# Turning softmax probabilities with VectorE and DRAM transfers instead of TensorE in a two-layer decoder trunk

## The chip, the core and the metric

The kernel runs on one core of a Trainium2 chip. The metric is device microseconds of one execution, from the core's first instruction to its last, with what lies around it. The core has five engines with queues of their own: TensorE (PE in the profile, with its weight loads as PEld), VectorE (DVE), ScalarE (ACT), GpSimd (POOL) and SyncE (SP), and 16 DMA engines that all queues share.

## The reference

Two pre-norm residual layers on one sequence of 256 tokens with 1024 features, in float32. Layer 0 mixes tokens by causal attention with forget gates, layer 1 by block-sparse attention with a learned relative bias, which for 256 tokens is one causal block. After each mixer come a SwiGLU feed-forward part of width 2816 and a gated per-layer embedding; a last RMS norm closes.

```python
probs = jax.nn.softmax(logits, axis=-1).astype(v.dtype)      # 16 heads, 256 queries, 256 keys
return jnp.einsum('bhqk,bhkd->bhqd', probs, v)               # 64 features of a head
...
h = h + _merge_heads(o) @ fox_w_o[j]
u = _rmsnorm(h, ffn_norm_g[i])
gu = u @ ffn_w_in[i]
h = h + (jax.nn.silu(gu[..., :D_FF]) * gu[..., D_FF:]) @ ffn_w_out[i]
gate = jax.nn.sigmoid(_rmsnorm(h, ple_norm_g[i]) @ ple_w_gate[i])
h = h + gate * (p[i] @ ple_w_up[i])
```

## The kernel before

Weights stream from DRAM once, in pieces of 128 partitions by 1024 values ("half", called by "blocks"; "gapped" reads a piece with a gap, 1080 values). SyncE issues the load into a tile "raw" (six buffers). ScalarE rounds it into "whi" (L163, L181), VectorE subtracts to get the remainder "wlo" (L165, L182); both have six buffers. A product is three matmuls, whi by x-hi, whi by x-lo and wlo by x-hi (mm3, L91 to L93), so that float32 is kept.

The 16 heads are worked in eight pairs, 0 to 7; a pair is 128 features. In attention a loop over j = 0, 2, 4, 6 does this on TensorE: it projects pairs j and j+1 (queries and keys, 96 matmuls, "pq"), and between the projections it does the attention steps of earlier pairs.

- scores (L506): query by key products of a pair ("sp"), then on VectorE the bias and the row minimum (L528), on ScalarE the exponential (L532), on VectorE the reciprocal (L535) and the scaling (L538). The probabilities of a pair lie in a tile "e" (four buffers), 128 queries by 2 heads by 384 columns: 128 keys for the first half of the queries, 256 for the second.
- transposes (L544): the value product needs keys on the partitions, so TensorE turns every 128 by 128 square of e (three a head, six a pair, L551) into a PSUM bank "pp", and ScalarE copies it to "pt" (L556).
- values (L559): pt by v ("po", L565 and L567), then "split" writes hi and remainder of the pair's output (o, L284 on ScalarE and L285 on VectorE).
- wo (L602): the output projection, in eight pieces of weights; piece (hf, c) needs the outputs of pairs 2c and 2c+1. wo(0, 0) and (1, 0) come behind the last scores.

The framework puts each engine's instructions in order ahead of the run, from what is ready by its own estimate, with the order of the program as priority; issue_after keeps named instructions behind others on their engine. On the chip each engine then works strictly in that order and waits where an operand is late. A new tile waits until the tile that held its buffer has been read for the last time.

GpSimd has almost nothing to do in attention, and no transfer is issued by it.

The steps of the last part of attention before, in the order of TensorE: projections of pairs 6 and 7, transposes of 3 and 4, values of 1 and 2, values of 3, scores of 5 and 6, scores of 7, wo(0, 0) and wo(1, 0), transposes of 5, wo(0, 1), transposes of 6 and 7, wo(1, 1), values of 4 and 5, values of 6 and 7, the rest of wo.

Of the kernel before, what the change touches and what calls it, by code (L numbers as in the profile page):

```python
# [27 lines left out]
F32 = mybir.dt.float32  # L28
F32R = mybir.dt.float32r
AF = mybir.ActivationFunctionType  # L30
ALU = mybir.AluOpType

P = 128
S = 256
# [4 lines left out]
NP = H // 2  # L39
# [10 lines left out]
WARM = 8  # L50
RAW = 6
RVW = 384


LINE = 64
# [17 lines left out]
def trunk(ctx: ExitStack, tc: tile.TileContext, xg, wx, xr, pt, w, cst, gf, rel, hot, rvm, out):  # L73
    nc = tc.nc
    one = ctx.enter_context(tc.tile_pool(name="one", bufs=1))
    work = ctx.enter_context(tc.tile_pool(name="work", bufs=2))
    tiny = ctx.enter_context(tc.tile_pool(name="tiny", bufs=2))
    ps = ctx.enter_context(tc.tile_pool(name="ps", bufs=8, space=bass.MemoryType.PSUM))
    dram = ctx.enter_context(tc.tile_pool(name="dram", bufs=1, space=bass.MemoryType.DRAM))
# [7 lines left out]
    mm = nc.tensor.matmul  # L87
# [184 lines left out]
    rr = tiny.tile([2 * BUCKETS, P], F32R, bufs=1, name="rr")  # L272
    ht = work.tile([2 * BUCKETS, RVW], F32, tag="e", bufs=4, name="ht")
    hot2 = work.tile([2 * BUCKETS, RVW], F32R, tag="e", bufs=4, name="hot2")
    rm = work.tile([H, RVW], F32, tag="e", bufs=4, name="rm")

# [4 lines left out]
    v = one.tile([P, 2, D], F32, name="v")  # L281
# [106 lines left out]
    def moba_bias():  # L388

        pb = bank("pb")  # L390
        mm(pb[:, :RVW], rr, hot2, start=True, stop=True)
        rv = work.tile([H, RVW], F32, tag="e", bufs=4, name="rv")
# [33 lines left out]
    def attention(layer, nm, mid, early, nf):  # L426
        vb = [bank(f"v{layer}_{b}") for b in range(4)]
        rest, ahead = None, []
        for c in range(4):
            wt = [early.pop(0) if early else half() for _ in range(2)]  # L430
            for kk in range(2):
                hi, lo = wt[kk]
                k = 2 * c + kk
                if layer == 0:
                    got = enter(vb, nm.k(k), wt[kk], k)
                for t in range(2 * layer):
                    for hf in range(2):
                        cols = slice(hf * HC, (hf + 1) * HC)
                        got = tokens(vb[2 * t + hf], nm.k(k), t, (hi[:, cols], lo[:, cols]), k == 0, k == KT - 1)
# [37 lines left out]
        qk, sm = {}, {}  # L477
# [3 lines left out]
        def project(j, a):  # L481
            if ahead:
                hi, lo = ahead.pop(0)
            elif j > 2 and (j % 2 == 0 or layer and j == 5) and a == 0 or layer and j == 4:
                hi, lo = gapped()
            else:
                hi, lo = blocks(ENTRY if layer and j in (0, 2) and a == 0 else ())
            if a == 0:
                pq[j] = bank(f"pq{layer}_{j}")
            bk = pq[j]  # L490
            for k in range(KT):
                mm3(bk[:, a * S:(a + 1) * S], (hi[k], lo[k]), nm.k(k),
                    start=(k == 0), stop=(k == KT - 1))
            if a == 0:
                return
            del pq[j]
            t = work.tile([P, 2, S], F32, tag="qkt", bufs=3, name=f"qkt{layer}_{j}")
            nc.vector.tensor_tensor(t.rearrange("p a s -> p (a s)"), bk,
                                    nm.row.rearrange("p a s -> p (a s)"), op=ALU.mult)

            th = work.tile([P, 3 * P], F32R, tag="qkh", bufs=3, name=f"qkh{layer}_{j}")
            tl = work.tile([P, 3 * P], F32R, tag="qkl", bufs=3, name=f"qkl{layer}_{j}")
            split(th, tl, t.rearrange("p a s -> p (a s)")[:, P:])
            qk[j] = t, th, tl

        def scores(*js):  # L506

            rows = [slice(s * DH, (s + 1) * DH) for s in range(2)]
            heads = [(2 * j + s, d, qk[j], bank(f"sp{layer}_{2 * j + s}")) for j in js for s, d in enumerate(rows)]
            for _, d, (t, _, _), sp in heads:  # L510
                mm(sp[:, 0:P], t[d, 0, 0:P], t[d, 1, 0:P], start=True, stop=add is None, skip_group_check=True)
            for n, (q, k) in enumerate(((1, 1), (1, 2), (2, 1))):
                for _, d, t, sp in heads:
                    got = mm(sp[:, P:3 * P], t[q][d, 0:P], t[k][d, P:], start=False, stop=(n == 2 and add is None),
                             skip_group_check=True)
            if add:
                for i, _, _, sp in heads:
                    got = add(i, sp)
            sl = (slice(0, P), slice(P, 3 * P))
            for n, j in enumerate(js):  # L520
                del qk[j]
                e = work.tile([P, 2, 3 * P], F32, tag="e", bufs=4, name=f"e{layer}_{j}")

                mn = tiny.tile([P, 2, 2, 2], F32, tag="mn", bufs=4, name=f"mn{layer}_{j}")
                for s in range(2):
                    i, _, _, sp = heads[2 * n + s]
                    for q, b in enumerate(bias(i)):
                        nc.vector.tensor_tensor_reduce(e[:, s, sl[q]], sp[:, sl[q]], b, 1.0, 3.0e38,  # L528
                                                       ALU.add, ALU.min, mn[:, 0, s, q:q + 1])
                for s in range(2):  # L530
                    for q in range(2):
                        nc.scalar.activation(e[:, s, sl[q]], e[:, s, sl[q]], AF.Exp, scale=-1.0,  # L532
                                             bias=mn[:, 0, s, q:q + 1], accum_out=mn[:, 1, s, q:q + 1])
                rc = tiny.tile([P, 2, 2], F32, tag="rc", bufs=4, name=f"rc{layer}_{j}")
                nc.vector.reciprocal(rc, mn[:, 1])  # L535
                for q in range(2):
                    at = e[:, :, sl[q]]
                    nc.vector.tensor_tensor(at, at, rc[:, :, q:q + 1].to_broadcast(list(at.shape)), op=ALU.mult)  # L538
                sm[j] = e
            return got  # L540

        pts = {}

        def transposes(j, tag="pt"):  # L544

            e = sm.pop(j)
            for s in range(2):
                i = 2 * j + s
                pp = bank(f"pp{layer}_{i}")
                for q in range(3):  # L550
                    got = nc.tensor.transpose(pp[:, q * P:(q + 1) * P], e[:, s, q * P:(q + 1) * P], ident)  # L551
                if tag == "pt":
                    pts[i] = work.tile([P, 3 * P], F32, tag="pt", bufs=4, name=f"pt{layer}_{i}")
                else:
                    pts[i] = work.tile([P, 2 * S], F32, tag="fp", bufs=4, name=f"pt{layer}_{i}")[:, 0:3 * P]
                nc.scalar.activation(pts[i], pp[:, 0:3 * P], AF.Copy)  # L556
            return got

        def values(*js):  # L559

            pos = [bank(f"po{layer}_{j}") for j in js]
            heads = [(slice(s * DH, (s + 1) * DH), slice((2 * j + s) * DH, (2 * j + s + 1) * DH), pts.pop(2 * j + s), po)
                     for j, po in zip(js, pos) for s in range(2)]
            for d, c, t, po in heads:
                mm(po[d, :S], v[:, 0, c], t[:, 0:S], start=True, stop=False, skip_group_check=True)  # L565
            for d, c, t, po in heads:
                got = mm(po[d, P:S], v[:, 1, c], t[:, S:], start=False, stop=True, skip_group_check=True)  # L567
            for j, po in zip(js, pos):
                split(oh[:, j], ol[:, j], po[:, :S])
            return got  # L570


        homes = ("pt", "fp") if layer else ("fp", "pt")
        for j in range(0, NP, 2):
            for i in (j, j + 1):
                project(i, 0)
                project(i, 1)
            if j == NP - 2:
                for i in (NP - 5, NP - 4):
                    transposes(i, homes[0])  # L580
                values(NP - 7, NP - 6)
                values(NP - 5)
                scores(NP - 3, NP - 2)
                end = scores(NP - 1)
            else:
                turned = layer == 1 and j == 4
                if turned:
                    for i in range(j - 3, j - 1):
                        transposes(i, "fp")
                if j >= 4:  # L590
                    values(*range(max(j - 5, 0), j - 3))
                got = scores(*range(max(j - 1, 0), j + 1))
                if j >= 2 and not turned:
                    for i in range(max(j - 3, 0), j - 1):
                        transposes(i)
            if layer == 0 and j == 0:
                with tc.issue_after(got.ins):
                    moba.extend(moba_bias())
# [7 lines left out]
        def behind(ins, *parts):  # L606
            with tc.issue_after(ins.ins):
                for a in parts:
                    wo(*a)

        behind(end, (0, 0), (1, 0))
        behind(transposes(NP - 3, homes[1]), (0, 1))
        transposes(NP - 2, homes[1])
        behind(transposes(NP - 1, homes[0]), (1, 1))
        values(NP - 4, NP - 3)
        behind(values(NP - 2, NP - 1), (0, 2), (1, 2), (0, 3))
        for hf in range(2):
            if hf:
# [232 lines left out]
    for layer in range(2):  # L851
# [5 lines left out]
        got = []  # L857
# [120 lines left out]
```

## Time and profile before

| what | value |
|---|---|
| median of 3 runs | 648.08 us (647.97 to 648.86) |
| the profiled execution | 648.17 us, span 646.4 us |
| TensorE clock granted | 0.999 |
| TensorE busy | 638.6 us, 99% of the span |
| VectorE, ScalarE, GpSimd busy | 455.0, 374.6, 10.6 us |
| DMA | 124.23 MB, mean 192 GB/s |

The span reaches from the first to the last instruction in the profile. TensorE's busy time is modelled from pipelined matmuls, so what a group of matmuls costs is read from the starts in the chain or the timeline and not from the mean duration of one.

### The profile page before, as it was taken

To read this page: it belongs to the slowest core of one execution; us is meant where nothing else is said; L and a number is where in the kernel's file an instruction comes from. 1 tells how busy PE (TensorE), PEld (TensorE's weight loads), DVE (VectorE), ACT (ScalarE), POOL (GpSimd) and SP (SyncE) were. 2 spreads that over 40 slices of the span, in tenths; PEclk is the share of its full clock that TensorE was granted. 3 is DMA by queue.
4 is the path that set the end of the run, shared out by engine and by line. 5 is a ranking of instruction groups with operands and counts; after the bars stand their busy time and mean duration, and the time that the engine had idled before them with its cause. 6 is when DMAs were issued, how large, how long until landed. Compare 5 with 4: busy or idle time off the path is not lost.

```text
span 646.4 us, 13196 instructions
## 1 busy us (share of the span) xinstructions
PE 638.6 (99%) x5373; PEld 617.8 (96%) x5373; DVE 455.0 (70%) x733; ACT 374.6 (58%) x635; POOL 10.6 (2%) x23
## 2 busy tenths in 40 slices
PE   9999999999999999999999999999999999999995
PEld 7899999999999999999989999999999999999985
DVE  7789875786666666659895888577666666666675
ACT  6686675754444445448665677666444444454763
POOL 0100000000000000000000000000000000000000
PEclk9999999999999999999999999999999999999999
DMA  9855544398765566565577554436666666665501
GB/s 341 306 197 185 159 128 154 104 328 277 249 201 196 192 194 215 184 206 191 195 242 280 175 166 135 131 106 212 215 196 195 197 198 197 199 210 195 166 1 65
DMA packets 36092, 124.23 MB, mean 192 GB/s; under 512 B 3936, under 2 KB 6592, under 8 KB 36032
## 3 DMA queue, kind: packets, MB, share of 16 engines
q1 hardware_dynamic: 35600, 122.77, 57.9%
q8 instruction: 42, 0.69, 0.4%
q10 hardware_dynamic: 432, 0.62, 0.3%
q14 instruction: 18, 0.15, 0.1%
HBM read 122.30 MB, written 4.22 MB: 196 GB/s over the span
## 4 chain that ended last, share of the span: by engine, by line
PE 97%; issue 2%; POOL 0%; POOLq 0%; DVE 0%; DVEq 0%
PE gu L91 12%; PE gu L92 12%; PE gu L93 12%; PE fo L93 6%; PE fo L91 6%; PE fo L92 6%; PE pq L91 5%; PE pq L93 5%; PE pq L92 5%; PE v L422 4%; PE wo L91 2%; PE wo L93 2%; PE wo L92 2%; PE pp L551 2%; PE pg L91 2%
## 5 line engine op out<-in xcount | busy, mean ns | idle before, releaser
L165 DVE TENSOR_TENSOR wlo<-raw,whi 128x1024 fp32r<-128x1024 f32 (+1 forms) x166 | 201.0, 1217 | 85.0 <-ACT whi L163 79.4
L163 ACT ACTIVATE whi<-raw 128x1024 fp32r<-128x1024 f32 x164 | 172.4, 1059 | 122.6 <-issue 52.6
L91 PE MATMUL gu<-g,whi 128*128 128x256 f32 x704 | 194.9, 277 | 0.0
L92 PE MATMUL gu<-g,whi 128*128 128x256 f32 x704 | 194.7, 277 | 0.0
L93 PE MATMUL gu<-g,wlo 128*128 128x256 f32 x704 | 194.5, 276 | 0.0
L93 PEld LDWEIGHTS gu<-g,wlo 128*128 128x128 f32 x704 | 132.3, 188 | 0.0
L92 PEld LDWEIGHTS gu<-g,whi 128*128 128x128 f32 x704 | 132.2, 188 | 0.1
L91 PEld LDWEIGHTS gu<-g,whi 128*128 128x128 f32 x704 | 132.2, 188 | 0.0
L93 PE MATMUL fo<-fp,wlo 128*128 128x256 f32 x352 | 97.4, 277 | 0.0
L91 PE MATMUL fo<-fp,whi 128*128 128x256 f32 x352 | 97.3, 276 | 0.0
L92 PE MATMUL fo<-fp,whi 128*128 128x256 f32 x352 | 97.3, 276 | 0.0
L182 DVE TENSOR_TENSOR wlo<-raw,whi 128x1080 fp32r<-128x1080 f32 x44 | 56.4, 1282 | 42.0 <-ACT whi L181 41.3
L91 PE MATMUL pq<-g,whi 128*128 128x256 f32 x256 | 71.3, 279 | 0.0
L181 ACT ACTIVATE whi<-raw 128x1080 fp32r<-128x1080 f32 x44 | 48.5, 1103 | 38.9 <-PE gu L92 27.1
L93 PE MATMUL pq<-g,wlo 128*128 128x256 f32 x256 | 70.8, 277 | 0.0
L92 PE MATMUL pq<-g,whi 128*128 128x256 f32 x256 | 70.8, 276 | 0.0
L92 PEld LDWEIGHTS fo<-fp,whi 128*128 128x128 f32 x352 | 66.2, 188 | 0.0
L91 PEld LDWEIGHTS fo<-fp,whi 128*128 128x128 f32 x352 | 66.1, 188 | 0.0
L93 PEld LDWEIGHTS fo<-fp,wlo 128*128 128x128 f32 x352 | 66.1, 188 | 0.0
L91 PEld LDWEIGHTS pq<-g,whi 128*128 128x128 f32 x256 | 48.1, 188 | 0.6 <-issue 0.2
L92 PEld LDWEIGHTS pq<-g,whi 128*128 128x128 f32 x256 | 48.1, 188 | 0.1
L93 PEld LDWEIGHTS pq<-g,wlo 128*128 128x128 f32 x256 | 48.1, 188 | 0.0
(187 smaller groups left out, 989.2 us busy)
## 6 DMA issues: line engine op xcount, KB each, us to landing
raw<-w SPq DMA_DIRECT2D x169, 512.0 KB, 4.2
raw<-w SPq DMA_DIRECT2D x44, 540.0 KB, 3.8
d<-d SPq DMA_DIRECT2D x4, 768.0 KB, 7.2
bias<-d SPq DMA_DIRECT2D x4, 512.0 KB, 7.0
hw<-wx SPq DMA_DIRECT2D x1, 640.0 KB, 6.0
hw<-xr SPq DMA_DIRECT2D x1, 640.0 KB, 7.6
p<-pt SPq DMA_DIRECT2D x2, 256.0 KB, 3.6
end<-gf SPq DMA_DIRECT2D x1, 512.0 KB, 4.3
```

The lines of the kernel that those rows point to most:

```text
L91: mm(o, ah, bh, start=start, stop=False, skip_group_check=True)
L92: mm(o, ah, bl, start=False, stop=False, skip_group_check=True)
L93: return mm(o, al, bh, start=False, stop=stop, skip_group_check=True)
L163: state["hi"] = state[f"hi{i}"] = nc.scalar.activation(hi[:, c], raw[:, c], AF.Copy)
L165: nc.vector.tensor_tensor(lo[:, c], raw[:, c], f32(hi[:, c]), op=ALU.subtract)
L181: nc.scalar.activation(ht, raw[:, 0:WW], AF.Copy)
L182: nc.vector.tensor_tensor(lt, raw[:, 0:WW], f32(ht), op=ALU.subtract)
L422: got = mm(bks[2 * t + hf], x[a][:, t * P:(t + 1) * P], w[b][:, hf * HC:(hf + 1) * HC], start=k + a + b == 0, stop=k + b == KT, skip_group ...
L551: got = nc.tensor.transpose(pp[:, q * P:(q + 1) * P], e[:, s, q * P:(q + 1) * P], ident)
```

## The change

Pairs 0 to 4 of each layer are no longer turned by TensorE. Behind the scaling of e, VectorE turns every 32 by 32 block in place within its 32 partitions (two instructions a pair) and lays the blocks out in a new tile t, which takes one of the four e buffers. GpSimd then writes t to DRAM in one transfer (128 rows of 3 KB, 384 KB) and reads it back in four (32 partitions each, runs of 768 bytes, 96 KB each), so that the blocks land on the partitions of their keys. Pairs 5, 6 and 7 are turned by TensorE as before. The tile pt now holds a whole pair and has two buffers (four of one head before), so that the reads of pair 2 wait for the values of pair 0, and those of pairs 3 and 4 for the values of 1 and 2. The value products read pt in runs of 32 columns.

In the loop the values of pairs 1 and 2 stay in the pass of j = 6; values of 3 move behind the transposes of 5 and are joined with those of 4, and wo(0, 1) is tied behind them; values of 5 are on their own. In the order of the program the last part is now: projections of 6 and 7, values of 1 and 2, scores of 5 and 6, scores of 7, wo(0, 0) and wo(1, 0), transposes of 5, values of 3 and 4, wo(0, 1), transposes of 6 and of 7, wo(1, 1), values of 5, values of 6 and 7, the rest of wo.

```diff
+TURNED = 5
...
-                sm[j] = e
+                if j < TURNED:
+                    turn(j, e)
+                else:
+                    sm[j] = e
...
+        def turn(j, e):
+            t = work.tile([P, 4, 3, 2, 32], F32, tag="e", bufs=4, name=f"turn{layer}_{j}")
+            for s in range(2):
+                nc.vector.transpose(t[:, :, :, s].rearrange("p c b x -> p b c x"),
+                                    e[:, s].rearrange("p (b c x) -> p b c x", b=3, x=32))
+            d = dram.tile([P, 6 * P], F32, name=f"dt{layer}_{j}")
+            nc.gpsimd.dma_start(d, t.rearrange("p c b s x -> p (c b s x)"))
+            p = work.tile([P, 4, 3, 2, 32], F32, tag="pt", bufs=2, name=f"pt{layer}_{j}")
+            for i in range(4):
+                nc.gpsimd.dma_start(p[32 * i:32 * i + 32].rearrange("p c b s x -> p c (b s x)"),
+                                    bass.AP(tensor=d.tensor, offset=d.offset + 192 * i,
+                                            ap=[[6 * P, 32], [32 * 6 * P, 4], [1, 192]]))
+            for s in range(2):
+                pts[2 * j + s] = p[:, :, :, s].rearrange("p c b x -> p b c x")
...
-                    pts[i] = work.tile([P, 3 * P], F32, tag="pt", bufs=4, name=f"pt{layer}_{i}")
+                    if s == 0:
+                        both = work.tile([P, 2, 3 * P], F32, tag="pt", bufs=2, name=f"pt{layer}_{j}")
+                    t = both[:, s]
...
-                mm(po[d, :S], v[:, 0, c], t[:, 0:S], start=True, stop=False, skip_group_check=True)
+                mm(po[d, :S], v[:, 0, c], t[:, 0:2], start=True, stop=False, skip_group_check=True)
...
-                got = mm(po[d, P:S], v[:, 1, c], t[:, S:], start=False, stop=True, skip_group_check=True)
+                got = mm(po[d, P:S], v[:, 1, c], t[:, 2], start=False, stop=True, skip_group_check=True)
...
+            if j >= 4:
+                values(*range(max(j - 5, 0), j - 3))
+            got = scores(*range(max(j - 1, 0), min(j + 1, NP - 1)))
             if j == NP - 2:
-                for i in (NP - 5, NP - 4):
-                    transposes(i, homes[0])
-                values(NP - 7, NP - 6)
-                values(NP - 5)
-                scores(NP - 3, NP - 2)
                 end = scores(NP - 1)
-            else:
-                turned = layer == 1 and j == 4
-                if turned:
-                    for i in range(j - 3, j - 1):
-                        transposes(i, "fp")
-                if j >= 4:
-                    values(*range(max(j - 5, 0), j - 3))
-                got = scores(*range(max(j - 1, 0), j + 1))
-                if j >= 2 and not turned:
-                    for i in range(max(j - 3, 0), j - 1):
-                        transposes(i)
...
-        behind(transposes(NP - 3, homes[1]), (0, 1))
-        transposes(NP - 2, homes[1])
-        behind(transposes(NP - 1, homes[0]), (1, 1))
-        values(NP - 4, NP - 3)
+        transposes(NP - 3, "fp")
+        behind(values(3, 4), (0, 1))
+        transposes(NP - 2, "fp")
+        behind(transposes(NP - 1), (1, 1))
+        values(NP - 3)
         behind(values(NP - 2, NP - 1), (0, 2), (1, 2), (0, 3))
```

More of the change, by code (lines that the diff above doesn't have):

```diff
@@ L552, in transposes @@
                 if tag == "pt":
-                    pts[i] = work.tile([P, 3 * P], F32, tag="pt", bufs=4, name=f"pt{layer}_{i}")
-                else:
-                    pts[i] = work.tile([P, 2 * S], F32, tag="fp", bufs=4, name=f"pt{layer}_{i}")[:, 0:3 * P]
-                nc.scalar.activation(pts[i], pp[:, 0:3 * P], AF.Copy)
+                    if s == 0:
+                        both = work.tile([P, 2, 3 * P], F32, tag="pt", bufs=2, name=f"pt{layer}_{j}")
+                    t = both[:, s]
+                else:
+                    t = work.tile([P, 2 * S], F32, tag="fp", bufs=4, name=f"pt{layer}_{i}")[:, 0:3 * P]
+                nc.scalar.activation(t, pp[:, 0:3 * P], AF.Copy)
+                pts[i] = t.rearrange("p (b c x) -> p b c x", b=3, x=32)
             return got
@@ L570, in values @@
             return got
-        homes = ("pt", "fp") if layer else ("fp", "pt")
         for j in range(0, NP, 2):
```

## The prediction

> **What bounds the kernel now.** First the page's top: busy shares by engine, then the summary of the chain that ended last. The columns of the first are busy time, share of the span, instructions.
>
> ```profile
> span 646.4 us, 13196 instructions
> PE 638.6 (99%) x5373; PEld 617.8 (96%) x5373; DVE 455.0 (70%) x733; ACT 374.6 (58%) x635; POOL 10.6 (2%) x23
> PE 97%; issue 2%; POOL 0%; POOLq 0%; DVE 0%; DVEq 0%
> ```
>
> TensorE is the bound, and 97% of the chain is its own work one after another: an instruction taken off it shortens the span unless a wait takes its place. The execution took 648.17 us, 1.8 us around its span; the median of the runs is 648.08 us, so both bases are the same within 0.1 us.
>
> Next the chain in order of time (start us, length us, what), at the end of attention in layer 0 (81 to 93 us) and in layer 1 (399 to 408 us). Length here is the time between starts, which is the price on TensorE.
>
> ```profile
> 66.33 0.58 PE po L565 x4
> ...
> 81.27 1.31 PE pp L551 x12
> 82.58 1.01 PE po L565 x8
> 83.59 0.44 PE po L567 x8
> 84.03 0.43 PE po L565 x4
> 84.68 0.65 PE sp L511 x8
> ...
> 87.14 0.32 PE wo L91
> 92.82 0.66 PE pp L551 x6
> ...
> 399.34 0.65 PE sp L511 x8
> ...
> 407.13 0.66 PE pp L551 x6
> ```
>
> The reader is to see that TensorE goes from transposes to values to scores to wo without a gap, so each step has its operand in time today.
>
> **The change part by part.**
>
> *Transposes that go.* Twelve take 1.31 us, 0.109 us each. Pairs 0 to 4 have six each, in two layers: 60 x 0.109 = 6.55 us off TensorE. All of a layer's thirty stand ahead of the values of pairs 1 and 2 (82.58 us), so from there on everything is 3.3 us earlier. The 20 copies of ScalarE behind them go too:
>
> ```profile
> L556 ACT ACTIVATE pt<-pp 128x384 f32<-128x384 f32 x32 | 13.2, 482 | 0.4 <-PE pp L551 0.4
> L285 DVE TENSOR_TENSOR qkl<-qkt,qkh 128x384 fp32r<-128x384 f32 x16 | 8.8, 551 | 0.0
> ```
>
> 20 x 0.48 = 9.6 us of ScalarE, off the path: nothing on TensorE waits for them but values.
>
> *VectorE's block transposes.* 20 instructions of 128 x 384. No row shows one. From below the 128 x 384 copy above, 0.48 us; from above twice the two-input row L285, 1.10 us, should the block write be slow. I take L285's 0.55 us, same engine, same size: 5.5 us a layer (4.8 to 11). What hides it is VectorE's lead with the weights:
>
> ```profile
> 41.10:54.60 13.50, 13.50 (x132) 12.88 (x128) 13.08 (x24) 8.49 (x17) 0.00 (x0) 1.00 0.84 268
> 54.60:68.80 14.20, 14.20 (x137) 13.51 (x135) 12.49 (x32) 9.54 (x25) 0.00 (x0) 1.00 0.58 180
> 68.80:82.60 13.80, 13.80 (x124) 13.60 (x124) 10.96 (x31) 10.19 (x26) 0.00 (x0) 1.00 0.47 144
> 47.26 1.03 DVE L538 TENSOR_TENSOR e<-e,rc 128x256 f32<-128x256 f32 x2
> 59.84 1.03 DVE L538 TENSOR_TENSOR e<-e,rc 128x256 f32<-128x256 f32 x2
> 64.81 1.28 DVE L182 TENSOR_TENSOR wlo<-raw,whi 128x1080 fp32r<-128x1080 f32 x1
> 69.34 0.28 DVE L528 CUSTOM_DVE_ANT_0 e<-sp,con 128x128 f32<-128x128 f32 x1
> 73.53 1.03 DVE L538 TENSOR_TENSOR e<-e,rc 128x256 f32<-128x256 f32 x2
> ```
>
> The stretches (window, length, then busy of PE, PEld, DVE, ACT, POOL, clock, DMA share, GB/s) give VectorE 36.5 us busy of 41.5. With 5.5 more in 38.2 it would be 3.8 us behind. But the third gapped remainder of the layer, at 64.81 us, is that of wo(0, 0) (the first two are pairs 4 and 6), and TensorE starts wo at 87.14: 21 us of lead, so 3.8 us (or 9.3 at the upper price) cost TensorE nothing. The same row shows that an engine's order follows what is ready and not the program alone: the wo piece stands ahead of the row minima of pair 3 (69.34).
>
> *GpSimd's transfers.* Five a pair, 50 in all, 7.9 MB beside 124. GpSimd is idle in attention (0.00 in all three stretches), so they queue behind nothing but each other. Two prices are not in the trace, since no transfer is issued by GpSimd: its time for one issue, and its landing. The nearest rows are SyncE's issues through DRAM (ns min/median/max) and its small transfers (KB, us to landing):
>
> ```profile
> L400 SPq DMA_DIRECT2D d<-d x4: 475/478/532, 128.3 to 172.1; - x4
> L406 SPq DMA_DIRECT2D bias<-d x4: 382/588/1432, 331.4 to 333.1; - x4
> gx<-xg ACTq DMA_DIRECT2D x1, 96.0 KB, 3.1
> out<-end SPq DMA_DIRECT2D x2, 128.0 KB, 2.1
> raw<-w SPq DMA_DIRECT2D x169, 512.0 KB, 4.2
> ```
>
> Issue: 0.59 us from below (the median of the reads from DRAM), 1.43 us from above (their longest). I take the middle, 1.0 us: GpSimd's issue should be no cheaper than SyncE's, and its small arithmetic is dear, as quoted below. Landing: 3.1 us, the row of 96 KB, the size of one read (2.1 to 4.2).
>
> ```profile
> L242 POOL TENSOR_TENSOR col<-ms,nhalf 128x2 f32<-128x2 f32 x6 | 5.9, 984 | 598.0 <-DVE ms L240 598.0
> L535 DVE RECIPROCAL rc<-mn 128x4 f32<-128x4 f32 x16 | 2.8, 176 | 3.3 <-ACT e L532 3.1
> ```
>
> The Trainium skill, "DMA: Bandwidth & Descriptors" (Latency and other measured facts), puts the first byte of a GpSimd transfer at about 1 us against 0.6 us for SyncE, and fits 2.0 us plus size over 436 GB/s to one transfer (Anatomy of one DMA), an estimate of 2.2 us for 96 KB; with these figures the wait worked out below would be 0.6 us a layer, and the sum 643.4 us. The same page (Issuing engine by pattern) would give plain transfers to SyncE; no run here shows a GpSimd transfer yet.
>
> *Pairs 0 to 2: covered.* Scaling of pair 0 ends at 48.3 us and of pair 2 at 60.9 (the L538 rows above). A round trip is write 1.0 + 4.2, reads 3 x 1.0 + 3.1: 11.3 us. Pair 0 has until its values at 66.33 us. Pairs 1 and 2 have until 82.58, and the reads of 2, which wait for the values of 0, still have some 15 us.
>
> *Pairs 3 and 4: the place that decides.* Scaling ends at 74.6 us (73.53 + 1.03), VectorE's two pairs of transposes add 2.2, GpSimd's two writes land near 82 minus 0.65, the part of the 3.3 us already saved there. The pt buffers come free at the end of the values of 1 and 2, 84.03 before and 80.8 after. So the reads start at about 81. The values of 3 and 4 now stand behind scores, wo(0, 0), wo(1, 0) and the transposes of 5: from 84.68 to 92.82 + 0.66 = 8.8 us in layer 0, from 399.34 to 407.13 + 0.66 = 8.45 us in layer 1. Eight reads need 7 x 1.0 + 3.1 = 10.1 us. They are 1.3 and 1.65 us late: +2.95 us. Behind the waiting product on TensorE stand wo(0, 1) and all that follows, so nothing fills the wait, unless the order puts the transposes of 6 (0.66 us) ahead; I count no such help.
>
> *wo(0, 1) behind the values of 3.* Its first twelve matmuls use pair 2, the others wait for the split of 3:
>
> ```profile
> L284 ACT ACTIVATE o<-po 128x256 fp32r<-128x256 f32 x16 | 5.4, 389 | 1.8 <-PE po L567 1.8
> L285 DVE TENSOR_TENSOR o<-po,o 128x256 fp32r<-128x256 f32 x16 | 6.0, 418 | 1.5 <-ACT o L284 1.5
> L163 ACT ACTIVATE whi<-raw 128x1024 fp32r<-128x1024 f32 x164 | 172.4, 1059 | 122.6 <-issue 52.6 <-PE gu L92 32.4 <-PE wo L92 9.7
> L92 PE MATMUL wo<-o,whi 128*128 128x256 f32 x128 | 35.4, 277 | 0.0
> ```
>
> 0.39 + 0.42 us, plus up to 1.06 if ScalarE has just begun a weight piece, against twelve matmuls (starts about 0.113 us apart, from the 5.68 us between 87.14 and 92.82 for 48 and two loads of weights: 0.118): 1.4 us. From 0 to 0.5 us a layer; I take 0.3, 0.6 in all.
>
> *Value products on runs of 32 columns.* No row shows TensorE reading such a pattern. From below 0; from above the double of L565 (0.43 us a pair) for ten pairs, 4.3 us. I take 0: runs of 128 bytes are long beside one column, and the row nearest is the dense one.
>
> *Sum.* 648.17 - 6.55 + 2.95 + 0.6 = 645.2 us, against the median 2.9 us or 0.4% faster.
>
> **The rivals.**
>
> *Hidden altogether.* With SyncE's 0.59 us an issue, eight reads need 7 x 0.59 + 3.1 = 7.2 us, under 8.45. Then 648.17 - 6.55 = 641.6 us, to 642.2 with the split. For it: the median row of SyncE. Against: GpSimd's arithmetic is five times VectorE's at a smaller size (984 against 176 ns).
>
> *The reads come late (slower than before).* One mechanism: GpSimd's queue is strict, and the write of pair 4 stands behind the reads of 3, which wait for pt. Then after the release come four reads (4.0), the write (landing 4.2) and four reads (3.0 + 3.1): 14.3 us, 5.5 and 5.85 us late, 648.17 - 6.55 + 11.35 + 0.6 = 653.6 us. Longer issues do the same: 7 x 1.43 + 3.1 = 13.1 us gives 651.2. It decides from a wait of 3.0 us a layer, that is a last landing 11.6 us behind the release, or 1.2 us an issue. For it: the program has the reads of 3 ahead of the write of 4, and one SyncE read did take 1.43. Against: the row at 64.81, ready work is placed first, and the write of 4 is ready some 3 us before the buffers are free. The Trainium skill, "SBUF — State Buffer" (the box on "DVE blocks DMA"), states that GpSimd cannot write descriptors while VectorE holds their shared port in a two-port operation, which would lengthen the issues just so. It says the same of two-input operations only against a GpSimd operation that reads, and those are most of VectorE's work here; no trace of this case shows either.
>
> *About even.* Waits of 2 to 3.5 us a layer, or value products at a part of their upper price: 646.8 to 649.4 us.
>
> *VectorE becomes the bound.* Only if its 21 us of lead went; at 9.3 us of lag at the most it does not. I give it nothing of its own.
>
> **How the numbers follow.** Chances: the sum, small waits (643.0 to 646.8) 0.42; hidden (641.0 to 643.0) 0.25; about even 0.10; late (649.4 to 656) 0.23. A measurement of this kernel tells 0.2%, 1.3 us, from no change. Faster: 0.42 + 0.25 = 0.67; same 0.10; slower 0.23. The likeliest is 645.2 us, with a range of its own of 643.0 to 646.8; the range over all cases is 641.4 to 654.0, which leaves out some 0.05 below and 0.1 above.
>
> **What would show it.** The transposes' group L551 at 36 instead of 96; VectorE's block transposes near 0.55 us x 20; a wait of about 1.5 us on TensorE's weight load or matmul at L565, released by a DMA, once a layer between the transposes of 5 and wo(0, 1); GpSimd's eight reads in a row behind the values of 1 and 2, about 1 us apart. In the chain, transfers or GpSimd's queue with some 3 us. The prediction is wrong if GpSimd's issues are far from 1.0 us, if a write stands between the reads of 3 and 4, or if the value products of pairs 0 to 4 are longer than those of 5 to 7.

## The result and the profile after

The kernel got slower. Medians: 652.2 us after (651.05 to 652.4, four runs) against 648.14 us before (647.97 to 648.86); the ratio is 1.006, with a 95% interval from 1.0049 to 1.0072. The forecast was 645.2 us and faster. The profiled execution took 652.05 us, with a span of 650.3 us against 646.4.

First the page of after: busy time, share and instructions of the engines, and the summary of the chain that ended last. Lines of the changed part stand 1 to 23 lines lower than in the kernel before (L498 is now L499, L551 is L571, L565 is L588).

```profile
span 650.3 us, 13157 instructions
PE 637.5 (98%) x5313; PEld 614.3 (94%) x5313; DVE 462.1 (71%) x753; ACT 367.0 (56%) x615; POOL 38.4 (6%) x73
PE 90%; issue 4%; DVE 2%; DMA 2%; POOL 1%; ACT 0%; POOLq 0%; DVEq 0%; ACTq 0%
```

TensorE was 97% of the chain and is 90%: other engines now set the time somewhere. The next two fences are the chain in order of time (start, length, what; pieces under 0.1 us left out), at the end of attention in layer 0 and in layer 1.

```profile
80.73 3.11 DMA dt<-turn
83.84 0.93 issue
84.77 1.63 POOL pt L558 x3
86.40 7.52 DMA pt<-dt
93.92 0.20 issue
94.12 0.65 PE po L588 x4
```

```profile
395.73 0.29 DVE e L539
396.06 0.69 DVE e L539
396.75 1.20 DVE wlo L183
397.94 0.95 DVE turn L552 x2
398.89 0.57 DVE qkt L499
399.46 0.66 DVE o L286 x2
400.13 0.50 DVE qkl L286
400.67 0.50 PE sp L515 x4
```

In layer 0 the chain runs through GpSimd's round trip of pair 4 and joins TensorE at the values of 4 (94.12). In layer 1 it is VectorE's queue, one instruction behind the other, up to the scores of pair 7: those need qkt (L499) and qkl (L286) of 7, and a piece of weights (L183) and the block transposes of 4 (L552) stand ahead of them. TensorE's view shows the one wait for the reads in layer 0, and the two for VectorE in layer 1:

```profile
94.12 0.65 PE L588 MATMUL po<-pt,v 128*64 128x256 f32 x4 [1.39 <-DMA pt<-dt]
...
399.52 0.49 PE L512 MATMUL sp<-qkt 64*128 64x128 f32 x4 [1.42 <-DVE qkt L499]
...
400.67 0.38 PE L515 MATMUL sp<-qkl,qkh 64*128 64x256 f32 x2 [0.21 <-DVE qkl L286]
```

VectorE's own timeline of that place before and after, in layer 0, shows how it came to be late. Before, it took qkt of 7 right when the projection had ended, and stood idle for 0.37 us ahead of it. After, the projection ends at 80.0 us and qkt is taken at 82.71.

```profile
81.31 0.69 DVE L498 TENSOR_TENSOR qkt<-pq,row 128x512 f32<-128x512 f32 x1 [0.37 <-PE pq L93]
```

```profile
72.82 0.18 DVE L536 RECIPROCAL rc<-mn 128x4 f32<-128x4 f32 x1 [1.10 <-ACT e L533]
73.03 1.03 DVE L539 TENSOR_TENSOR e<-e,rc 128x256 f32<-128x256 f32 x2
74.09 1.04 DVE L552 STREAM_TRANSPOSE turn<-e 128x384 f32<-128x384 f32 x2
75.06 0.25 DVE L529 CUSTOM_DVE_ANT_0 e<-sp,con 128x128 f32<-128x128 f32 x1
...
79.41 1.03 DVE L552 STREAM_TRANSPOSE turn<-e 128x384 f32<-128x384 f32 x2
80.36 2.43 DVE L183 TENSOR_TENSOR wlo<-raw,whi 128x1080 fp32r<-128x1080 f32 x2
82.71 0.68 DVE L499 TENSOR_TENSOR qkt<-pq,row 128x512 f32<-128x512 f32 x1
```

Three things add up: 2.07 us of block transposes in the pass (one turn of the loop, with the softmax of two pairs); the row minima of pair 4 (75.06) now stand behind pair 3's scaling and transposes, so that VectorE stands idle for 1.10 us while ScalarE does the exponentials of 3; and the remainders that were hidden work come in between. Before, all eight minima stood in a row, from 69.34 (a row of the prediction) to 71.64 us.

The two busy tables (busy of PE, PEld, DVE, ACT, POOL, clock, DMA share, GB/s) show the stretch in which TensorE should do the scores of 5 to 7, and the clock after it:

```profile
396.67:401.10 4.43, 2.74 (x33) 2.02 (x31) 4.43 (x9) 1.29 (x4) 2.75 (x5) 1.00 0.90 261
```

```profile
398.00:399.00 1.00, 0.10 (x2) 0.00 (x0) 1.00 (x3) 0.00 (x0) 1.00 (x2) 1.00 0.82 226
399.00:400.00 1.00, 0.48 (x4) 0.30 (x4) 1.00 (x3) 0.50 (x1) 0.60 (x2) 1.00 1.01 228
400.00:401.00 1.00, 0.73 (x8) 0.48 (x6) 1.00 (x3) 0.02 (x1) 0.00 (x0) 1.00 1.04 310
...
402.00:403.00 1.00, 1.00 (x7) 1.00 (x6) 1.00 (x9) 0.95 (x5) 0.00 (x0) 0.52 0.84 249
...
405.00:406.00 1.00, 1.00 (x8) 1.00 (x8) 0.89 (x7) 1.00 (x7) 0.00 (x0) 0.78 0.07 29
```

VectorE is busy for all of the 4.43 us, TensorE for 2.74. After three microseconds in which TensorE was busy for 1.31, its granted clock falls to half, from 402.0 to 405.4 us (3.41 us, see the last section), and wo(0,0) and wo(1,0) take 7.30 us instead of 5.76.

The whole account, from the starts of TensorE's stages in both traces (us, after less before):

| where | us |
|---|---|
| 60 transposes gone: stages of 3.38 in layer 0 and 3.43 in layer 1 | -6.81 |
| scores of 5 to 7: layer 0 2.46 to 4.19, layer 1 1.95 to 4.42 | +4.20 |
| half clock in layer 1 (wo 5.76 to 7.30) | +1.54 |
| values of 3 and 4: 3.07 and 1.88, against 1.45 for those of 1 and 2 | +2.05 |
| two trains of 96 products in layer 0 at a wider spacing | +0.94 |
| from the last matmul to the end of the span: 6.99 to 7.77 | +0.78 |
| the rest (transposes of 5 +0.5, a third group of value products +0.3, other trains) | +1.20 |
| span, 646.4 to 650.3 | +3.90 |

A train is a run of products of one stage, one behind the other; the wider spacing is 117.8 instead of 113.3 ns from start to start.

### The profile page after: what moved, and what is told of

Read it like the earlier page. It is cut to its first block, busy times and chain, and to the rows that moved or that the text cites. A ratio compares the mean times of both kernels' runs of the same rounds, so it can differ in the third digit from the quotient of the medians.

```text
span 650.3 us, 13157 instructions
## 1 busy us (share of the span) xinstructions
PE 637.5 (98%) x5313; PEld 614.3 (94%) x5313; DVE 462.1 (71%) x753; ACT 367.0 (56%) x615; POOL 38.4 (6%) x73
## 4 chain that ended last, share of the span: by engine, by line
PE 90%; issue 4%; DVE 2%; DMA 2%; POOL 1%; ACT 0%; POOLq 0%; DVEq 0%; ACTq 0%
PE gu L92 12%; PE gu L93 12%; PE gu L94 12%; PE fo L94 6%; PE fo L92 6%; PE fo L93 6%; PE pq L92 4%; PE v L423 4%; PE pq L93 4%; PE pq L94 4%; PE wo L92 2%; PE wo L93 2%; PE wo L94 2%; PE pg L92 2%; PE pg L93 2%
## 5 line engine op out<-in xcount | busy, mean ns | idle before, releaser
L183 DVE TENSOR_TENSOR wlo<-raw,whi 128x1080 fp32r<-128x1080 f32 x44 | 56.2, 1279 | 42.2 <-ACT whi L182 42.2
```

What stands on the lines that cost most here:

```text
L183: nc.vector.tensor_tensor(lt, raw[:, 0:WW], f32(ht), op=ALU.subtract)
```

## The experiments

The theory, V: VectorE is late for pair 7. The rival, R: the reads through DRAM land late, and that is the loss. A third candidate is a fixed price of the transfers. Each time below is a median beside the kernel before on the same chip, with the ratio and its interval. The kernel before took 647.91 to 648.23 us on these chips and 648.14 beside after, so a difference to after (652.2 us) is good to some 0.3 us.

| run | us | before | ratio |
|---|---|---|---|
| e1 no reads | 650.09 | 647.91 | 1.003 [1.0019, 1.004] |
| e2 no block transposes | 644.98 | 647.91 | 0.9953 [0.994, 0.9965] |
| e3 fill | 650.61 | 647.91 | 1.0038 [1.0025, 1.0052] |
| e4 minima first | 647.99 | 647.91 | 1.0004 [0.9995, 1.0012] |
| e5 before, with blocks | 649.99 | 648.23 | 1.0028 [1.0019, 1.0037] |
| e6 before, with transfers | 650.47 | 648.23 | 1.0041 [1.0029, 1.0054] |
| e7 values later | 648.11 | 648.23 | 0.9999 [0.9991, 1.0008] |
| e8 four turned | 647.25 | 648.23 | 0.9986 [0.9977, 0.9995] |
| e9 four, one transpose | 646.86 | 647.95 | 0.9984 [0.9975, 0.9993] |
| e10 three turned | 648.46 | 647.95 | 1.0006 [0.9997, 1.0015] |
| e11 scaling on ScalarE | 648.67 | 648.1 | 1.0013 [1.0004, 1.0022] |
| e12 both | 650.58 | 648.1 | 1.0039 [1.0026, 1.0053] |

**e1, no reads.** The round trip is taken out of the kernel after:

```
-            d = dram.tile([P, 6 * P], F32, name=f"dt{layer}_{j}")
-            nc.gpsimd.dma_start(d, t.rearrange("p c b s x -> p (c b s x)"))
...
-                pts[2 * j + s] = p[:, :, :, s].rearrange("p c b x -> p b c x")
+                pts[2 * j + s] = v[:, 0, 0:3 * P].rearrange("p (b c x) -> p b c x", b=3, x=32).bitcast(F32)
```

> Leaves out all 50 transfers of GpSimd: the values of pairs 0 to 4 are multiplied by a tile that lies ready (other data); the block transposes of VectorE stay. Theory V (VectorE is late with qkt and qkl of pair 7, which TensorE's scores of 7 wait for, and the idle halves the clock in layer 1): the scores of 5 to 7 keep their 1.7 and 2.5 us of excess, only the waits for reads (1.6 + 0.4) and the longer end (0.8) go: 652.2 - 2.8 = 649.4 us. Theory R (the late reads are the cause, and VectorE's lag would be covered): about 648.1 - 6.55 = 641.6 us, up to 643.

Measured 650.09 us, 2.1 less than after. The waits of the scores stay as they were, without a single transfer of GpSimd (TensorE's waits: us in total, times, longest):

```profile
PE sp L512 <- DVE qkt L499: 1.5, 2, 1.4
PE sp L515 <- DVE qkl L286: 0.8, 2, 0.6
```

The scores of 5 to 7 take 4.15 and 4.37 us, and the half clock is there again. R falls as the main cause; the late reads and the end are worth 2 us, as V has it. The end from last matmul to end of span is 6.98 us again.

**e2, no block transposes.** L550 to L553 go, the tile t among them, and the write takes e:

```
-            t = work.tile([P, 4, 3, 2, 32], F32, tag="e", bufs=4, name=f"turn{layer}_{j}")
...
-            nc.gpsimd.dma_start(d, t.rearrange("p c b s x -> p (c b s x)"))
+            nc.gpsimd.dma_start(d, e.rearrange("p s x -> p (s x)"))
```

> Leaves out the turning inside the blocks: GpSimd writes e itself, VectorE makes no block transposes. Theory V: the scores of 5 to 7 fall back to about 2.5 and 2.0 us, the clock stays at 1.00 in layer 1; in layer 0 the reads still land near 93 us, so that a part of what is won is waited for there: 652.2 - 2.5 - 1.5 - (0 to 1.7) = 646.5 to 648.2 us. Theory R: the reads land as late as before the edit, no more than 0.5 us: 651.7 us or more.

Measured 644.98 us: 7.2 us less than after, more than V had expected, and within 0.2 us of the time forecast for the change. The scores take 2.45 and 1.95 us, the clock stays at 1.00, and no wait for a read is left. The reads were late because of VectorE: without the block transposes both writes of the last pass are issued before the buffers come free, at 386.72 and 388.47 us, and the eight reads follow in one go (GpSimd's timeline, layer 1, first this run, then after):

```profile
388.47 0.56 POOL L551 DMA_DIRECT2D dt<-e  x1 [1.19 <-ACT whi L182]
394.48 4.38 POOL L554 DMA_DIRECT2D pt<-dt  x8 [5.45 <-PE po L586]
```

```profile
392.69 0.56 POOL L555 DMA_DIRECT2D dt<-turn  x1 [1.52 <-DVE mn L529]
396.85 2.19 POOL L558 DMA_DIRECT2D pt<-dt  x4 [3.60 <-PE po L590]
399.18 0.56 POOL L555 DMA_DIRECT2D dt<-turn  x1
406.06 2.19 POOL L558 DMA_DIRECT2D pt<-dt  x4 [6.32 <-PE wo L94]
```

In layer 1 of after the write of 4 stands behind the reads of 3, and the reads of 4 wait for its landing; in layer 0 it is issued at 80.73 us, just ahead of the reads of 3 (81.63). The run takes out more than the load, though: without t VectorE also has its eight row minima in a row again (69.15 to 71.4 us in layer 0). e4 and e11 hold the two apart.

**e3, wo(0,0) as a filler** between the scores of 6 and those of 7:

```
...
-        behind(end, (0, 0), (1, 0))
+        behind(got, (0, 0))
+        end = scores(NP - 1)
+        behind(end, (1, 0))
```

> Order alone: wo(0,0) goes between the scores of 5, 6 and those of 7, so 2.8 us of TensorE's work lie where it waited for VectorE. Theory V: the wait for qkt and qkl of 7 goes, and the half clock with it: 5.7 us won ahead of the values of 3 and 4, but the last read lands at the same time, so in layer 0 1.7 of it is waited for again: 652.2 - 4.0 = 648.2 us (646.5 if the reads move too). Theory R: nothing won, 652 us.

Measured 650.61 us; 648.2 was a miss. The profile is of the longest execution, 652.94 us against 650.51 to 650.71 us of the other four, so its waits are larger than those behind the median. In it the gap was only partly filled, since wo(0,0) needs VectorE too (its splits of o stand in the same queue). And what was won there was waited for at the reads of 4 in layer 1, still issued behind a write that stood behind the reads of 3:

```profile
PE po L588 <- DMA pt<-dt: 3.2, 1, 3.2
```

So work for TensorE in the gap doesn't mend it: the queue of VectorE and the chain behind it are late themselves.

**e4, minima first.** Program order alone: both pairs' minima and exponentials, then both pairs' scaling and turn.

```
+                es[j] = e, mn
+            for j in js:
+                e, mn = es[j]
                 rc = tiny.tile([P, 2, 2], F32, tag="rc", bufs=4, name=f"rc{layer}_{j}")
```

> Program order alone: the row minima and exponentials of both pairs of a pass stand ahead of the scaling and block transposes of the first. Theory V with the held-back minima as its main part: VectorE wins the 1.1 us a pass in which it waited for ScalarE, the scores of 7 wait about 1 us less in each layer, and the half clock may go: 652.2 - 2 to 3.5 = 648.7 to 650.2 us. Theory V with the 2 us of block transposes as its main part: under 0.7 us won, 651.5 us or more. Theory R: the writes of 3 come later, 652.2 us or more.

Measured 647.99 us: 4.2 us less than after and even with the kernel before, more than any branch had given. The scores take 2.45 us in layer 0 and 3.06 in layer 1, no half clock, and both writes are issued ahead of the reads. The 1.1 us a pass in which VectorE stood idle thus cost 4.2 us in the two layers, since the half clock hangs on them too: the scores win 3.1 us and the clock 1.5, of which the last wo of layer 0 loses 0.4 at the wider spacing. At the values of 3 and 4 nearly as much is lost as in after (0.85 and 0.92 us, against 1.62 and 0.43), although the writes are early. What is left of the waits:

```profile
PE po L592 <- DMA pt<-dt: 1.5, 3, 0.7
PE sp L515 <- DVE qkl L286: 0.6, 1, 0.6
```

**e5, the kernel before with the block transposes added**, into e buffers that nobody reads.

> The kernel before with the 20 block transposes of VectorE added into e buffers that nobody reads; TensorE's transposes and everything else stay. Theory V says that VectorE's lag is what costs. In the order of before, 1.3 us of transposes and 0.65 of values of 3 stand between the projection of 7 and its scores, so some of the 2 us a pass is covered: +1 to +4 us, 649 to 652 us, with waits for qkt or qkl of 7. The prediction on record (VectorE's lead covers it) says 648.1 us.

Measured 649.99 us, +1.8. In layer 1 the projection of 7 ends at 396.96 us and VectorE takes qkt 2.3 us later:

```profile
399.23 0.68 DVE L498 TENSOR_TENSOR qkt<-pq,row 128x512 f32<-128x512 f32 x1
```

In after it is 3.6 us late (395.22 to 398.81). The scores of 5 to 7 lose 2.5 us there in after and 0.43 us here, where 1.40 us of transposes and 0.65 us of values of 3 still stand between the projection and the scores: in layer 1 the change took away work that covered a part of VectorE's lag. Layer 0 says nothing on this, since TensorE had itself been held up and VectorE had caught up (qkt 0.2 us behind the projection's end, no loss at the scores). Another 1.2 us are lost at an earlier place of layer 0, where TensorE waits for a bank of PSUM behind a late split of o:

```profile
70.28 0.55 PE L561 MATMUL pp<-con,e 128*128 128x128 f32 x3 [0.69 <-DVE o L285]
```

**e6, the kernel before with the transfers added**, e written and four reads into buffers that nobody uses.

> The kernel before with GpSimd's 50 transfers added (e written, four reads into buffers that nobody uses); no block transposes. If the end of the kernel grows by the queue that GpSimd's transfers bring, the time from the last matmul to the end of the span is 7.8 us as after, not 7.0, and the total is 648.9 us. If the transfers also hold up the weights, waits for weights appear and it is 650 us or more; the rival that transfers cost nothing gives 648.1 us.

Measured 650.47 us, +2.2. The end of the span grows to 7.77 us as in after, 0.78 us. The other 1.4 us are the same wait for a bank in layer 0 as in e5: pair 2 is scaled at 65.59 us instead of 59.84. VectorE's timeline shows a part of what holds it back: the row minima of 2 wait for the landing of a read, whose target has taken an e buffer:

```profile
62.53 0.29 DVE L528 CUSTOM_DVE_ANT_0 e<-sp,con 128x128 f32<-128x128 f32 x1 [1.82 <-DMA pt<-dt]
```

In after VectorE waits for no transfer in attention, so this price is e6's own. No wait for weights appeared.

**e7, minima first, and the values of 3 and 4 behind the transposes of 6.**

> Minima first as in the run before, and the values of 3 and 4 behind the transposes of 6 (wo(0,1) moves with them). If the 0.85 and 0.92 us that these values still wait are the reads' landing, 0.66 us of transposes fill them: 648.0 - 1.3 = 646.7 us. If something else holds them (VectorE's scaling of 6, which the transposes need, comes late), the wait only changes its name: 648.0 us.

Measured 648.11 us, nothing won: the second branch. The wait only changes its name, from the reads to ScalarE's copies behind the transposes, which stand behind the exponentials of 7 and weight pieces:

```profile
PE po L592 <- ACT pt L582: 1.8, 2, 1.1
```

**e8, four pairs turned**, minima first:

```
-TURNED = 5
+TURNED = 4
...
+                transposes(4)
                 end = scores(NP - 1)
```

> Minima first; pairs 0 to 3 are turned by VectorE, pair 4 by TensorE as before, between the scores of 6 and those of 7. Against all five: 12 transposes more on TensorE (+1.3 us, of which the 0.3 and 1.1 us by which scores of 7 were late are filled), no second write and four reads fewer in front of the values of 3 and 4 (-0.9 and -0.9). Theory V with reads second: 648.0 + 1.3 - 1.1 - 1.8 = 646.4 us. If a fixed cost of the round trip (end of the kernel, spacing of the matmuls) is the rest: 647.5 us or more.

Measured 647.25 us, 0.14% faster than before, the interval just clear of 1. In the profile TensorE waits for no engine and no transfer in attention any more, so the 5.2 us of transposes that it saves should show. Most of them don't: the end takes 0.73 us of them, and trains of matmuls at the wider spacing 2.05 us more than before (some 800 starts against 340, 4.5 ns each). Scores of 7, transposes of 4 and 5 and the third group of value products take 0.5 us in layer 0 and 0.7 in layer 1 more than in the kernel before. That is -5.2 + 0.7 + 2.05 + 1.2 = -1.25, the difference of the spans (645.1 against 646.4).

**e9, e8 and four transposes of the identity more**, ahead of trains that had become slower.

> The run with four turned pairs, and four transposes of the identity into unused columns more: one behind the scores of 1, 2 and one behind those of 3, 4 of layer 0, one behind the values of 6, 7 of each layer, 0.11 us each. These places stand ahead of trains of 96 matmuls that run at 117.8 ns a start where transposes used to stand ahead of them and they ran at 113.3 ns. If what stands ahead of a train sets its spacing: the trains fall from 11.5 or 11.4 us to 11.1 or 11.0, some 1.7 us less in four trains, 0.44 us more for the transposes: 647.2 - 1.2 = 646.0 us. If the spacing goes by something else: 647.6 us.

Measured 646.86 us, the lowest of the kernels that leave nothing out, but within the interval of e8. One train of the four changed: the last wo of layer 0, from 11.41 us (starts 101.60 to 113.01) to 10.97 (101.57 to 112.54), and the first trains of gate and up products behind it with it. The two projections of layer 0 and the last wo of layer 1 did not (11.48, 11.48 and 11.38 us). What stands ahead of a train can change its spacing, but does not decide it; what does stays open.

**e10, three pairs turned**, minima first, pairs 3 and 4 by TensorE.

> Minima first; pairs 0 to 2 turned by VectorE, pairs 3 and 4 by TensorE, between the scores of 6 and those of 7. Against four turned: 12 transposes more on TensorE (+1.3 us), no block transpose in the last pass, no transfer near the values of 3 and 4. In the run with four no wait of TensorE was left that these edits could take away, so: 647.2 + 1.3 = 648.5 us. If VectorE's last block transposes still held up the scores of 7 or the transposes of 5 to 7 (the stages stood 0.2 us each above those of before): 647.9 us.

Measured 648.46 us, as the first branch has it: 12 transposes more cost their 1.2 us, and nothing else of e8 goes. The block transposes of one pair in the last pass cost nothing there.

**e11, scaling of pairs 0 to 4 on ScalarE**, in the order of after:

```
+                if j < TURNED:
...
+                            nc.scalar.activation(at, at, AF.Copy, scale=rc[:, s, q:q + 1])
+                    turn(j, e)
+                    continue
```

> The kernel after, with the row scaling of pairs 0 to 4 moved from VectorE (1.03 us a pair) to ScalarE (four activations with a scale, about 1.4 us a pair; ScalarE has lost the 0.96 us a pair of copies); program order as it was. Theory V, load as its part: VectorE has 2.1 us less to do a pass, just what the block transposes added, so the scores of 7 come down by 1 to 2 us a layer and the half clock goes: 646.5 to 649 us. If the order of the minima is the whole of it, or ScalarE becomes late instead (qkh of 7): 651 us or more.

Measured 648.67 us, 3.5 less than after: VectorE's load is nearly as good a handle as its order. The scores take 3.08 and 4.11 us, so layer 1 wins only 0.3 us at its scores; in the profiled execution the clock stays whole, and wo(0,0) and wo(1,0) take 5.56 us.

**e12, both.**

> Both: scaling of pairs 0 to 4 on ScalarE and the minima of both pairs first. Against minima first alone (648.0 us) VectorE has 2.1 us less a pass: the scores of 7 lose their last 1.1 us of wait in layer 1, and turn, write and reads of 4 come up to 2 us sooner, which takes the 0.85 and 0.92 us of the values of 3 and 4: 645.2 to 646.0 us, the time of the run without block transposes. If ScalarE's longer queue takes it back: 647.5 us or more.

Measured 650.58 us, a miss of 5: the two remedies undo each other, by the last branch. With the minima first, ScalarE gets eight exponentials in a row and the scaling of 3 behind them, and VectorE waits for ScalarE, twice in a pass, ahead of the block transposes:

```profile
390.42 0.18 DVE L540 RECIPROCAL rc<-mn 128x4 f32<-128x4 f32 x1 [1.58 <-ACT e L534]
391.11 1.27 DVE L560 STREAM_TRANSPOSE turn<-e 128x384 f32<-128x384 f32 x2 [0.52 <-ACT e L545]
```

## Why the prediction was wrong, by its own steps

*Transposes that go, -6.55 us:* right, 36 are left, and the stages that went had taken 6.81 us. The price of 0.109 us from the chain was 0.26 us low over the 60.

*VectorE's block transposes at 0.55 us:* right as a price. The group's line (ns min/median/max) has 554 for the forecast of 0.55 us from the two-input row.

```profile
L552 DVE STREAM_TRANSPOSE turn<-e x20: 534/554/580, 48.8 to 398.4; 128x384 f32<-128x384 f32 x20
L558 POOL DMA_DIRECT2D pt<-dt x40: 552/552/573, 55.4 to 407.7; - x40
```

*"3.8 us cost TensorE nothing", "VectorE becomes the bound: I give it nothing of its own":* this is the step that failed. The lead of 21 us that it read at 64.81 is that of the weights' remainders alone. VectorE's queue also has qkt and qkl of pair 7, which have no lead: they are ready when the projection ends, and TensorE wants them behind the scores of 5 and 6 and 3.5 us of other work (1.40 of transposes, 2.10 of values), of which the change leaves 1.45 us. The kernel before had it in its own trace: at 81.31 us, the row quoted above, VectorE waits for the projection and has no lead at all. The margin had to be read at the work with the least lead, and the same edit shortened it by 2.05 us. After, qkt comes 2.7 us behind the projection in layer 0 and 3.6 us in layer 1, and TensorE loses 1.73 and 2.47 us at the scores and 1.54 at half clock. e1, e2, e4 and e11 show it from four sides; e5 shows the cover in layer 1. The order of VectorE was not foreseen either: the row minima of pair 4, ahead of the scaling of 3 before, fell behind its block transposes, and e4 puts 4.2 us on this alone, since the half clock hangs on it. e11 gains 3.5 us from VectorE's load alone, so the two overlap and are no parts of a sum.

*GpSimd's issues at 1.0 us:* they took 0.552 us, below the lower end. VectorE was busy without a break in the stretch quoted above, and the longest issue of a read took 0.573 us, that of a write 0.762. That write is the kernel's first transfer by GpSimd, and in e2, without block transposes, the first takes 0.762 us too. The Trainium skill, "SBUF — State Buffer" (the box on "DVE blocks DMA"), speaks of two-port operations of VectorE holding up GpSimd's descriptors; the trace shows no such stall, and not whether any of VectorE's operations here is of that kind.

*Landing at 3.1 us:* medians of 4.7 us for reads and 4.2 for writes, the longest read 8.65 us. The DMA engines' busy share is 0.8 to 1.1 in the stretches 82:91 and 397:402, where weights come in too. The Trainium skill, "DMA: Bandwidth & Descriptors" (Anatomy of one DMA), gave the estimate of 2.2 us for 96 KB; the reads of layer 1 at 406.06, with the engines nearly free, landed after 2.30 to 2.39 us, so it fits an idle queue and not this one.

```profile
dt<-turn POOLq DMA_DIRECT2D x10, 384.0 KB, 4.2
pt<-dt POOLq DMA_DIRECT2D x40, 96.0 KB, 4.7
```

*Reads late by 1.3 and 1.65 us:* 1.62 and 0.43 us were lost at the values of 3 and 4, 2.05 instead of 2.95. Near, but by luck, through errors that cancel: cheaper issues against longer landings, and reads that came later (the writes of 4 landed at 84.23 and 405.52 us, not at 81.4) against a TensorE that came later too, 10.6 and 12.5 us behind the start of the scores instead of 8.8 and 8.45. In layer 1 the write of 4 also stood between the reads of 3 and 4, the order of the slower rival and one of the prediction's own signs of being wrong. In e2 no wait for a read is left, so this loss too hung on VectorE.

*wo(0,1) behind the split, +0.6:* it takes 2.82 and 2.84 us before and 2.84 after; nothing was lost there.

*Value products on runs of 32 columns, 0:* right. The values of pair 0, before on dense columns and after on runs, take 0.80 us in both kernels and both layers.

*Not in the sum at all:* the half clock (+1.54), the end of the span (+0.78), and the spacing of the trains (+0.94 in two of them).

Put in one line: the transposes were right within 0.3 us, the reads came near by luck, and +5.7 us of VectorE's lateness with the clock behind it were set at nothing.

## What to carry to other kernels

When work is moved to an engine that has time on average, look for the instruction on it with the least lead, not the one with the most, and ask whether the same edit takes away the work that stood between its input and its consumer. Look also at the order: an instruction that follows a wait for another engine holds back everything that was ready, so put what can start first ahead of it; here that was worth 4.2 us, while adding a second remedy (e12) made a new wait. The best version found turns four pairs, minima first, and gains 0.14% (0.16% with e9's transposes, within the interval).

## What the runs showed of the hardware

- **The clock.** The granted clock of after was at half for 3.41 us (columns as in the busy tables above):

```profile
402.04:405.45 3.41, 3.41 (x19) 3.41 (x18) 3.41 (x20) 3.40 (x15) 0.00 (x0) 0.50 0.69 229
```

  Two stretches of the same length from the time before it, the second right ahead of it:

```profile
91.42:94.84 3.42, 1.99 (x20) 1.26 (x20) 2.98 (x5) 2.56 (x6) 0.00 (x0) 1.00 0.33 84
398.62:402.04 3.42, 2.25 (x18) 1.73 (x19) 3.42 (x9) 0.52 (x1) 0.98 (x2) 1.00 0.98 288
```

  In e1 (401.04 to 404.45) and e3 (409.81 to 413.22) the half clock lasted 3.41 us too, and in each of the three traces all changes of the clock lie whole multiples of 3.413 us apart (after: 6.09, 402.04, 405.45, 647.79). The two stretches lie on this grid. Behind the first, in which TensorE was busy for 1.99 us and idle for 1.39 in one piece, the clock stayed at 1.00. Behind the second, in which it was busy for 2.25 us and which holds 0.90 of the idle 1.42 us, the clock halved. So, by the busy time as the profile models it, neither the idle time of such a stretch nor its longest idle piece decides it, and what does stays open. In e3 an idle time of 3.15 us lies in the stretch ahead of the halving. The Trainium skill, "TensorE: Matmul & The Clock Gate" (Part 1: The HAM clock gate), has the clock halve after an idle window of some 3.4 us of a count that runs freely, and come back after a busy one. The 3.41 us and the even grid agree with that; but in after the array was not idle for the whole window, it was busy for 2.25 us of it.
- **Two spacings.** Trains of 256-column products run at 113.3 or at 117.8 ns from start to start, and most keep the one from the first few starts to the end: 10.9 to 11.1 or 11.4 to 11.5 us for 96. A train can change, though: the one at 370.06 us of the kernel before begins at the wider spacing and falls to the other after some 25 starts (11.13 us). It goes without transfers too (e1 has some 760 starts at the wider spacing, after 600, before 340). What picks it is open.
- **The end.** Any use of GpSimd's transfers made the end 0.72 to 0.78 us longer (e2, e3, e4 and e6 to e12 too), and without them (e1, e5) it was 6.98 us, against 6.99 before.
